# Feed-forward of a hybrid decoder layer: one set of PSUM tiles for both ways, weights loaded in quarters, a fifth room for stores, two operands of the way down loaded early

## The chip, the cores and the metric

The kernel runs on one core of a Trainium2 chip, in one launch. Its time is the device time in microseconds (us) of an execution, and the measure of a kernel is the median of its runs. A profile is one execution recorded by the hardware profiler; its span runs from the first to the last instruction.

## The reference, cut to what matters

One layer of a decoder works on 1024 prompt tokens and 8 sample tokens, each of 1024 features, in float32. A mixer (gated linear attention, a gated recurrence, windowed attention), cross-attention to a memory and a feed-forward block each add to `x`. The change lies in the last of them:

```python
D_MODEL, SEQ, DEC_BATCH, D_FF = 1024, 1024, 8, 4096

def ffn(x, g, w1, w2):
    h = rmsnorm(x, g) @ w1                      # 1024 -> 4096
    return jnp.square(jax.nn.relu(h)) @ w2      # 4096 -> 1024

xp = xp + ffn(xp, g_ffn[l], ffn_w1[l], ffn_w2[l])   # prompt
xs = xs + ffn(xs, g_ffn[l], ffn_w1[l], ffn_w2[l])   # sample
```

## The kernel before, in words

All tokens are taken together: N = 1032 columns, features on the partitions. A float32 product is made of three products of rounded operands: each operand is kept as a high and a low half (`halves`: ACT rounds the source into `hi`, DVE writes `lo = src - hi`), and TensorE adds `hi*hi`, `hi*lo` and `lo*hi` (`terms`).

The feed-forward runs in 30 units (`UNITS`). Hidden features 0 to 511 (the pairs p = 0 and 1 of 256 features) are computed plainly ahead of them, by `pl_cell`. Units 0 to 13 are the way up, one pair (p = 2 to 15) of hidden features each; units 14 to 29 are the way down, two (one for each half `dq` of the output features) for each of 8 chunks `c` of 512 hidden features. Both use a 2x2 scheme with seven products in place of eight, whose operands are named A11, S2, S1, A12, S3, S4, A21, A22 (weights and their sums) and B11, T2, B21, T1, T3, B22, T4 (data and its differences). The last names the steps too.

On the way up (`up_unit`) the 1032 columns form three groups of 344: the scheme makes two of them, in eleven groups of 12 products together with the third group, which is made plainly into `fe`. The results `fa` to `fg` go from PSUM to the cells `h` and three help cells in tile `gc` (ACT: relu and square; DVE: additions). Bank `fd` is filled by step S3, read by DVE and filled on by step A22. Each pair's `h` then gives seven operands for the way down; `h_store` splits each into halves in one of the rooms of `ST["ring"]` (two halves of a `q` tile, shown as `hst`, a part of a `v` tile, shown as `wsum`, and `MKV`) and stores it to DRAM (`hd`, 516 KB). A room is taken again when its last store has landed. For the last two pairs the ring has three rooms. `h_done` lists the stores of a pair: two are made in its own unit's step A22, five in the next unit through `bg_run`, which takes so many entries of a list at each step. The plain pairs' stores are spread over units 0 to 10 (`slow`).

On the way down (`down_unit`) the steps are A11, S2, A12, S1, S3, S4, A22, one operand each: `h_load` brings its two halves (516 KB each) from `hd` to a room of `RING`: parts of the operand tiles of the way up (`hs`, `ls`: shown as `xoph`, `xopl`) and of `XH`, `XL`, which come free as the last up unit ends. Each step has 24 products into tiles `a`, `b`, `c` or `d`. In the first chunk ACT copies a result to its place (`acc`, in tile `gc` at first, or `XT`), later DVE adds it there. A12 goes on with the tiles `a` of A11, S4 with `c` of S1, A22 with `d` of S3.

Weights: `unit_raw(n)` loads a unit's raw weights, 1 MB, to one of two tiles `wraw`; `unit_sums` makes the four sums on GpSimd (POOL); `prep(q)` splits one operand into halves (`wop`), five steps ahead (`LOOK`). The loads for unit n+1 are issued with the first split for unit n. All DMAs here are issued by SyncE (SP), in order. The program is ordered by Tile's scheduler; within an engine instructions run in that order.

PSUM: up to the last up unit there are tiles of four tags (`d`, `a`, `b`, `c`) in pool `psd`; ahead of unit 14 that pool is closed (`first_half.close()`) and pool `psy` opened over its place, with four tiles of two banks.

## Time and profile before

| | us |
|---|---|
| time of the kernel before, median of 3 runs | 1397.5 |
| lowest and highest run | 1393.65, 1398.03 |
| time of the profiled execution | 1394.97 |
| span of the profiled execution | 1393.3 |
| PE busy in it | 1322.7 |

The span is cut by the first product of each unit: `fa` on the way up, `a` on the way down. The first up unit begins at 745.77, the first down unit at 1051.35, the last at 1357.81. In a timeline row, the first number is the start, the second the duration, and the bracket at its end the time that the engine sat idle before it, with what ended that. DVE is VectorE, ACT ScalarE, PE TensorE, POOL GpSimd, SP SyncE, and SPq an issue of a DMA by SP. A row of a window has its start and end, its length, the busy time (and count of instructions) of PE, PE's weight loads, DVE, ACT and POOL, the granted clock as a share of full speed, the mean busy share of the 16 DMA engines, and GB/s. The helpers' lines are L141 (a product), L161 (ACT), L171 (DVE).

### The profile page before, as it was taken

What the parts mean: (1) busy time and instruction counts of PE and PEld (TensorE: products, weight loads), DVE (VectorE), ACT (ScalarE), POOL (GpSimd) and SP (SyncE); (2) the same over time, 40 slices, a digit from 0 to 9 for tenths busy, and PEclk for the clock granted to TensorE, in tenths of its full rate; (3) what the DMA queues carried; (4) which work ended last, traced back from release to release, by engine and by line L of the source; (5) the groups of instructions that cost most, each with busy time, mean ns of one, the idle gap of its engine ahead of it and who ended that gap; (6) DMA issues with size and microseconds to landing.
All of it is one profiled execution on the core that took longest, in us unless ns stands there. A gap on an engine that the chain in (4) does not pass through costs nothing.

```text
span 1393.3 us, 24517 instructions
## 1 busy us (share of the span) xinstructions
PE 1322.7 (95%) x9251; PEld 1216.9 (87%) x9251; DVE 1009.6 (72%) x1993; ACT 685.8 (49%) x1393; POOL 260.3 (19%) x245
## 2 busy tenths in 40 slices
PE   6999999999997989998999999999997999999998
PEld 4889888777876877786799999999997999999997
DVE  6276787667767664767698888878775577877785
ACT  5265455246476454555566676766664322222221
POOL 3000011400003101010004231322322223322310
PEclk9999999999998899998999999999999999999999
DMA  6114010201101444442243677676679988765624
GB/s 185 46 49 122 9 48 18 67 25 31 47 8 51 140 149 124 142 131 71 71 125 103 224 266 255 233 248 240 241 260 367 344 306 304 259 249 210 227 76 123
DMA packets 181022, 215.87 MB, mean 155 GB/s; under 512 B 26866, under 2 KB 114990, under 8 KB 180888
## 3 DMA queue, kind: packets, MB, share of 16 engines
q1 hardware_dynamic: 180264, 214.01, 45.8%
q8 instruction: 73, 1.20, 0.4%
q0 software_dynamic: 640, 0.30, 0.1%
q14 instruction: 45, 0.37, 0.1%
HBM read 145.28 MB, written 70.06 MB: 155 GB/s over the span
## 4 chain that ended last, share of the span: by engine, by line
PE 61%; DVE 17%; DMA 8%; ACT 8%; issue 4%; SPq 1%; POOL 0%; DVEq 0%; ACTq 0%; POOLq 0%
PE win L141 9%; PE a L141 7%; PE d L141 6%; PE c L141 6%; PE wo L141 6%; DMA hd<-hst 3%; PE b L141 3%; PE v L141 2%; PE f L141 2%; DMA hd<-wsum 2%; PE gx L141 2%; ACT hc L161 2%; DVE hc L171 2%; DVE hst L171 2%; PE wmo L141 2%
## 5 line engine op out<-in xcount | busy, mean ns | idle before, releaser
L1919 POOL TENSOR_TENSOR wsum<-wraw 128x512 f32<-128x512 f32 x60 | 86.7, 1445 | 389.1 <-DVE wop L171 312.2
L141 PE MATMUL win<-XL,wh 128*128 128x344 f32 x384 | 126.5, 330 | 0.0
L141 PE MATMUL win<-XH,wh 128*128 128x344 f32 x384 | 126.2, 329 | 0.2 <-ACT xy L161 0.2
L141 PE MATMUL win<-XH,wl 128*128 128x344 f32 x384 | 125.4, 327 | 0.0
L161 ACT ACTIVATE wh<-ws 128x512 fp32r<-128x512 f32 x130 | 79.9, 626 | 75.8 <-DMA ws<-in_w_out_dram 22.3
L141 PE MATMUL fe<-XH,wop 128*128 128x344 f32 x448 | 115.5, 321 | 0.0
L161 ACT ACTIVATE wop<-wsum 128x512 fp32r<-128x512 f32 x104 | 65.1, 626 | 97.7 <-PE d L141 29.8
L171 DVE TENSOR_TENSOR wl<-ws,wh 128x512 fp32r<-128x512 f32 x130 | 92.7, 725 | 28.0 <-ACT wh L161 23.3
L161 ACT ACTIVATE wop<-wraw 128x512 fp32r<-128x512 f32 x104 | 63.8, 625 | 96.7 <-PE b L141 32.7
L171 DVE TENSOR_TENSOR wop<-wsum,wop 128x512 fp32r<-128x512 f32 x104 | 80.5, 775 | 26.0 <-ACT wop L161 25.0
L171 DVE TENSOR_TENSOR wop<-wraw,wop 128x512 fp32r<-128x512 f32 x104 | 76.4, 735 | 10.1 <-ACT wop L161 9.5
L141 PEld LDWEIGHTS fe<-XH,wop 128*128 128x128 f32 x448 | 79.7, 190 | 0.0
L141 PEld LDWEIGHTS win<-XL,wh 128*128 128x128 f32 x384 | 72.2, 188 | 5.2 <-issue 3.9
L141 PEld LDWEIGHTS win<-XH,wl 128*128 128x128 f32 x384 | 72.3, 188 | 3.6 <-issue 2.7
L141 PEld LDWEIGHTS win<-XH,wh 128*128 128x128 f32 x384 | 72.2, 188 | 3.3 <-issue 1.9
L141 PE MATMUL fe<-XL,wop 128*128 128x344 f32 x224 | 71.9, 321 | 0.0
L141 PE MATMUL a<-XH,wop 128*128 128x258 f32 x352 | 67.6, 283 | 0.0
L141 PE MATMUL wo<-XH,wh 128*128 128x344 f32 x192 | 64.3, 335 | 2.2 <-ACT wh L161 2.2
L161 ACT ACTIVATE hc<-hc 128x344 f32<-128x344 f32 x126 | 61.3, 486 | 8.8 <-DVE hc L171 7.1
L141 PE MATMUL wo<-XH,wl 128*128 128x344 f32 x192 | 64.2, 334 | 1.0 <-DVE wl L171 1.0
L141 PE MATMUL wo<-XL,wh 128*128 128x344 f32 x192 | 63.0, 328 | 0.0
L141 PE MATMUL d<-XH,wop 128*128 128x258 f32 x320 | 60.8, 283 | 0.0
(547 smaller groups left out, 4123.9 us busy)
## 6 DMA issues: line engine op xcount, KB each, us to landing
wraw<-in_ffn_w_dram SPq DMA_DIRECT2D x60, 512.0 KB
hd<-hst SPq DMA_DIRECT2D x59, 516.0 KB
XH<-hd SPq DMA_DIRECT2D x36, 516.0 KB
XL<-hd SPq DMA_DIRECT2D x36, 516.0 KB
hd<-wsum SPq DMA_DIRECT2D x29, 516.0 KB
hd<-MKV SPq DMA_DIRECT2D x24, 516.0 KB
xoph<-hd SPq DMA_DIRECT2D x20, 516.0 KB
xopl<-hd SPq DMA_DIRECT2D x20, 516.0 KB
```

The costliest lines, as they stand in the source:

```text
L141: PE.matmul(out, lhsT, rhs, start=start, stop=stop, **kw)
L161: return ACT.activation(out, in_, func, **kw)
L171: return DVE.tensor_tensor(out, a, b, op=op)
L1919: POOL.tensor_tensor(o, a, b, op=op)
```

## The change

- PSUM: the first pool is closed ahead of unit 0, and four tiles of two banks, `Z["z"]`, serve the way up and the way down. On the way up `fa` takes tile 0, `fb`, `fc` and `fg` tile 1, `fe` tile 2, `fd` tile 3, each a bank of it in turn.
- Weights: `unit_raw` loads a unit's weights in four parts of 256 KB; `prep` issues them with the second to fifth split of the unit before instead of all with the first.
- Stores: a fifth room, of two `ws` tiles, from unit 1 on; a store from it is two DMAs of 258 KB. The last pair uses two rooms, the one before it three. On the way down two entries of the list of stores are taken at each step instead of one.
- Operands of chunk 0: B11 and T2 are loaded in unit 12 to a `q` and an `e` tile that are free by then; B21, T1, T3 and B22 in unit 13, T4 and three operands of chunk 1 in unit 14. The ring of rooms begins two operands later.
- The two output halves of chunk 0 are taken in the order 0, 1; the places of `acc` change with it. Three small tiles become one (`scales`), and `ws` tiles are 516 wide instead of 512.

```diff
-    UNITS = [...] + [("down", c, q) for c in range(NUNIT)
-                                                         for q in ((1, 0) if c == 0 else (0, 1))]
+    UNITS = [...] + [("down", c, q) for c in range(NUNIT) for q in range(2)]
...
-    def unit_raw(n):
+    def unit_raw(n, parts=range(4)):
...
-            for h in range(2):
-                SP.dma_start(r[:, 4 * h:4 * h + 4], w[:, 4 * h:4 * h + 4])
+            k = 2
...
-            for h in range(2):
-                SP.dma_start(r[:, 2 * h:2 * h + 2], w[:, 2 * h:2 * h + 2])
+            k = 1
+        for h in parts:
+            SP.dma_start(r[:, k * h:k * h + k], w[:, k * h:k * h + k])
...  prep(q)
-            if i == A11:
-                if n + 1 < len(UNITS):
-                    unit_raw(n + 1)
+            k = q - BASE[n]
+            if k == 0:
                 unit_sums(n)
+            elif k < 5 and n + 1 < len(UNITS):
+                unit_raw(n + 1, (k - 1,))
...  h_store(p, op, src)
-        ring_ = ST["ring"] if p < NPAIR - 2 else ST["ring"][:3]
+        ring_ = ST["ring"][:{NPAIR - 1: 2, NPAIR - 2: 3}.get(p)]
...
-        SP.dma_start(d, st.rearrange("p (s c) -> p s c", s=2))
+        if len(st) > 2:
+            SP.dma_start(d, v3(st[2], 2))
+        else:
+            for k in range(2):
+                SP.dma_start(d[:, k], st[k])
...  st_rooms()
-        ST["ring"] = [ST["q"][:, :N], ST["v"][:, 2048:2048 + N], ST["q"][:, N:], MKV]
+        ST["ring"] = [(x[:, :HALF], x[:, HALF:], x) for x in (ST["q"][:, :N], ST["q"][:, N:], ST["v"][:, 2048:2048 + N],
+                                                              MKV)]
...  up_unit(n)
-        def bank(f, name):
-            ps[name] = f(name)[:, :GW]
+        def bank(z, name):
+            h = Z["i", z] = 1 - Z.get(("i", z), 1)
+            ps[name] = Z["z"][z][:, 512 * h:512 * h + GW]
...
+            if n == 1 and i == A11:
+                ST["ring"].append([F("ws", HALF, "hst") for _ in range(2)])
+            if n == NPAIR - NPLAIN - 2:
+
+                if i == S2:
+                    for op, tag in ((B11, "q"), (T2, "e")):
+                        t = F(tag, 2 * N, "hfirst")
+                        HOP["r", op] = [v3(t[:, j * N:(j + 1) * N], 2) for j in range(2)]
+                elif i in (A12, A21):
+                    h_load(0, B11 if i == A12 else T2)
             if n == NPAIR - NPLAIN - 1:
 
-                for op in {S1: (B11, T2), S4: (B21,), A21: (T1,)}.get(i, ()):
+                for op in {S1: (B21, T1), S4: (T3,), A21: (B22,)}.get(i, ()):
                     h_load(0, op)
...  h_load(c, op)
-        kind, k, j = RING[(NOP * c + op) % len(RING)]
-        if kind == "x":
+        kind, k, j = RING[(NOP * c + op - 2) % len(RING)]
+        if (c, op) in ((0, B11), (0, T2)):
+            room = HOP["r", op]
+        elif kind == "x":
...  down_unit(n)
-        psP, psQ = (lambda name, tag=tag: psy.tile([128, 1024], F32, tag=tag, bufs=2, name=name)
-                    for tag in ("pr" if n % 2 else "rp"))
+        sets = [Z["z"][:2], Z["z"][2:]]
+        psP, psQ = sets[n % 2], sets[1 - n % 2]
...
-            bg_run(2 if k == 6 else 1)
+            bg_run(2)
...
-    for op in (T3, B22, T4):
-        at(d0, op - T3, lambda op=op: h_load(0, op))
+    at(d0, 0, lambda: h_load(0, T4))
...
-            at(*((d0 + 2 * c - 2 + n, k) if c > 1 else (d0 + 1, op)), lambda c=c, op=op: h_load(c, op))
+            at(*((d0 + 2 * c - 2 + n, k) if c > 1 or op > 1 else (d0, 2 + 3 * op)), lambda c=c, op=op: h_load(c, op))
...
-    psy = None
+    first_half.close()
+    psy = ctx.enter_context(tc.tile_pool(name="psy", bufs=1, space=bass.MemoryType.PSUM))
+    Z["z"] = [psy.tile([128, 1024], F32, name=f"z{i}") for i in range(4)]
     for n, u in enumerate(UNITS):
...
-        if n == d0:
-            first_half.close()
-            psy = ctx.enter_context(tc.tile_pool(name="psy", bufs=1, space=bass.MemoryType.PSUM))
```

## Rows read from the trace of the kernel before

**Rows 1.** The page: busy times, and PE's granted clock in 40 slices, in tenths.
```profile
PE 1322.7 (95%) x9251; PEld 1216.9 (87%) x9251; DVE 1009.6 (72%) x1993; ACT 685.8 (49%) x1393; POOL 260.3 (19%) x245
...
PEclk9999999999998899998999999999999999999999
```

**Rows 2.** Windows of units 5, 9, 12 to 15, 17; columns told above.
```profile
849.83:875.26 25.43, 22.72 (x135) 22.30 (x133) 21.20 (x32) 16.83 (x34) 6.85 (x5) 0.93 0.68 236
937.70:961.66 23.96, 21.02 (x134) 20.75 (x133) 19.25 (x28) 16.66 (x33) 6.22 (x4) 1.00 0.71 244
1003.29:1024.10 20.81, 20.81 (x134) 20.81 (x133) 16.91 (x24) 14.03 (x28) 7.69 (x5) 1.00 0.63 230
1024.10:1051.35 27.25, 21.23 (x134) 20.69 (x132) 18.50 (x28) 15.23 (x33) 6.03 (x5) 0.95 0.79 280
1051.35:1077.18 25.83, 23.95 (x178) 23.53 (x179) 15.43 (x21) 12.62 (x23) 6.17 (x4) 0.92 1.03 370
1077.18:1096.11 18.93, 18.93 (x161) 18.93 (x159) 8.02 (x11) 9.76 (x17) 4.61 (x4) 1.00 0.90 324
1116.24:1136.37 20.13, 20.13 (x170) 20.13 (x169) 15.53 (x23) 4.43 (x7) 5.17 (x5) 1.00 0.86 313
```

**Rows 3.** PE's waits from 745.7 on: us in total, times, longest.
```profile
PE fd L141 <- DVE hc L171: 6.4, 3, 2.9
PE a L141 <- ACT hc L161: 5.3, 1, 5.3
PE c L141 <- DMA xoph<-hd: 1.2, 1, 1.2
PE c L141 <- DMA xopl<-hd: 0.7, 1, 0.7
```

**Rows 4.** Timeline of unit 5: ACT and PE.
```profile
862.23 0.64 ACT L161 ACTIVATE hst<-hpl 128x516 fp32r<-128x516 f32 x1 [1.25 <-DMA hd<-hst]
863.86 0.64 ACT L161 ACTIVATE hst<-hc 128x516 fp32r<-128x516 f32 x1 [0.47 <-DMA hd<-hst]
...
869.87 0.40 PE L141 MATMUL fd<-XH,wop 128*128 128x344 f32 x1 [2.71 <-DVE hc L171]
```

**Rows 5.** ACT's waits for rooms in units 0 to 13.
```profile
ACT hst L161 <- DMA hd<-hst: 21.3, 13, 4.6
ACT wsum L161 <- DMA hd<-wsum: 16.4, 8, 3.5
...
ACT MKV L161 <- DMA hd<-MKV: 3.6, 4, 1.6
```

**Rows 6.** Timeline at the seam, ACT and PE, and of unit 14, ACT.
```profile
1049.42 0.63 ACT L161 ACTIVATE hst<-hc 128x516 fp32r<-128x516 f32 x1 [4.58 <-DMA hd<-hst]
...
1050.86 0.44 ACT L161 ACTIVATE hc<-fe 128x344 f32<-128x344 f32 x1
...
1051.35 0.58 PE L141 MATMUL a<-xoph,wop 128*128 128x258 f32 x1 [5.32 <-ACT hc L161]
...
1054.34 0.60 ACT L161 ACTIVATE gc<-a 128x516 f32<-128x516 f32 x1 [1.62 <-PE a L141]
...
1071.73 0.64 ACT L161 ACTIVATE hst<-hc 128x516 fp32r<-128x516 f32 x1 [2.66 <-DMA hd<-hst]
```

**Rows 7.** Timeline: issues of SP in units 5 and 13, POOL in unit 5.
```profile
861.06 2.00 SPq L1899 DMA_DIRECT2D wraw<-in_ffn_w_dram  x2
...
870.40 1.29 POOL L1919 TENSOR_TENSOR wsum<-wraw 128x512 f32<-128x512 f32 x1 [11.90 <-DVE wop L171]
...
1038.31 0.47 SPq L1959 DMA_DIRECT2D hd<-hst  x1
```

**Rows 8.** Window at the seam, with columns as in rows 2.
```profile
1044.00:1060.00 16.00, 10.68 (x69) 10.40 (x69) 8.85 (x13) 6.99 (x14) 5.70 (x4) 0.79 1.04 372
```

**Rows 9.** Timeline at the start of unit 0: PE, ACT.
```profile
745.77 0.32 PE L141 MATMUL fa<-XH,wop 128*128 128x344 f32 x1
...
746.40 0.44 ACT L161 ACTIVATE hpl<-f 128x344 f32<-128x344 f32 x1
```

More of the change, by code (lines that the diff above doesn't have):

```diff
@@ L513, in trunk_step @@
     spt = cst.tile([128, 4, 3], F32, name="spt")
-    qsc = cst.tile([128, 2], F32, name="qsc")
-    gkq = cst.tile([128, 2], F32, name="gkq")
-    gq8 = cst.tile([128, 2], F32, name="gq8")
+    scales = cst.tile([128, 6], F32, name="scales")
+    qsc, gkq, gq8 = (scales[:, i:i + 2] for i in (0, 2, 4))
     hgo = cst.tile([128, 3], F32, name="hgo")
@@ L1874, in trunk_step @@
     ST, HC, PL = {}, {}, {}
-    UNITS = [("up", p) for p in range(NPLAIN, NPAIR)] + [("down", c, q) for c in range(NUNIT)
-                                                         for q in ((1, 0) if c == 0 else (0, 1))]
+    UNITS = [("up", p) for p in range(NPLAIN, NPAIR)] + [("down", c, q) for c in range(NUNIT) for q in range(2)]
     RAW, SUM, OPS = {}, {}, {}
@@ L1888, in trunk_step @@
     BASE = [QUEUE.index((n, A11)) for n in range(len(UNITS))]
-    def unit_raw(n):
+    def unit_raw(n, parts=range(4)):
         u = UNITS[n]
-        if n < 2:
+        if n < 2 and parts[0] == 0:
             RAW["t", n] = F("q", 2048, "wraw")
@@ L2061, in up_unit @@
             if i == A11:
-                terms(bank(psA, "fa"), w, XOP[B11], True, False)
+                terms(bank(0, "fa"), w, XOP[B11], True, False)
                 with lift(LIFT_E):
                     act(p1, ps["fa"], AF.Copy)
-                terms(bank(psB, "fe"), w, XOP[GA][:4], True, False)
+                terms(bank(2, "fe"), w, XOP[GA][:4], True, False)
             elif i == A12:
@@ L2072, in up_unit @@
             elif i == S2:
-                terms(bank(psD, "fb"), w, XOP[T2], True, True)
+                terms(bank(1, "fb"), w, XOP[T2], True, True)
                 with lift(LIFT_E):
@@ L2076, in up_unit @@
             elif i == S1:
-                terms(bank(psD, "fc"), w, XOP[T1], True, True)
+                terms(bank(1, "fc"), w, XOP[T1], True, True)
                 with lift(LIFT_E):
@@ L2080, in up_unit @@
             elif i == S3:
-                terms(bank(psC, "fd"), w, XOP[T3], True, False)
+                terms(bank(3, "fd"), w, XOP[T3], True, False)
                 with lift(LIFT_E):
@@ L2086, in up_unit @@
             elif i == S4:
-                terms(bank(psD, "fg"), w, XOP[B22], True, True)
+                terms(bank(1, "fg"), w, XOP[B22], True, True)
                 with lift(LIFT_E):
@@ L2092, in up_unit @@
             elif i == A21:
-                terms(bank(psB, "fe"), w, XOP[GA][:4], True, False)
+                terms(bank(2, "fe"), w, XOP[GA][:4], True, False)
             else:
@@ L2133, in x_add @@
         tt(hv(XT[m], j), hv(XT[m], j), hv(ST["x", m], j), ADD)
+    Z = {}
     def y_rooms(dq):
@@ L2140, in y_rooms @@
                 XT[m], XT[m + 1] = t[:, :N], t[:, N:]
-            HC["acc", 1] = [HC["gt"][:, u * HALF:(u + 1) * HALF] for u in range(2)]
+            t = F("u", N, "acc")
+            HC["acc", 1] = [hv(t, u) for u in range(2)]
         else:
@@ L2146, in y_rooms @@
                 XT[m] = t[:, m * N:(m + 1) * N]
-            t = F("u", N, "acc")
-            HC["acc", 0] = [hv(t, u) for u in range(2)]
+            HC["acc", 0] = [hv(HC["gt"], u) for u in range(2)]
     def y_out(m, f):
-        p = f("yp")
+        p = f[m % 2]
         for h in range(2):
@@ L2211, in part, with banks @@
                       [(f32r(x[0])[:, k, cs], f32r(x[1])[:, k, cs]) for k in range(2)], start, stop)
-        def banks(f, name):
+        def banks(z, name):
             for u in range(2):
-                ps[name, u] = f(name)
+                ps[name, u] = z[u]
         for k, i in enumerate(seq(n)):
```

6 lines of the change are left out of this document (3 added, 3 removed).

## The prediction, written before the result

> **What bounds the kernel now.** Read the page first. PE is busy 95% of the span, and its granted clock stands at 9 tenths or more in all slices but the 13th, 14th and 19th, which lie in the first half, that the change leaves alone [rows 1]. So the kernel is PE's, and a change can only take away time in which PE waits, or in which it works at the lower of its two clock levels (1.2 instead of 2.4 GHz). Second, cut the feed-forward stage into its units [rows 2]. Units 0 to 13 are the way up, 14 to 29 the way down. Eleven of the fourteen up units last 20.81 us at a clock of 1.00 (unit 12 is shown), and a settled down unit lasts 20.13. The reader is to see which windows are longer:
>
> - unit 5: 25.43 - 20.81 = 4.62 us, at a clock of 0.93
> - unit 9: 23.96 - 20.81 = 3.15, at 1.00
> - unit 13: 27.25 - 20.81 = 6.44, at 0.95
> - units 14 and 15 together: 25.83 + 18.93 - 2 x 20.13 = 4.50, unit 14 at 0.92
>
> That is 18.7 us, and it is all that is to be had between the first up unit and the last down unit. Third, PE's waits in this stage [rows 3]: `fd` for DVE 6.4 in three waits, `a` for ACT 5.3, `c` for two loads 1.9, together 13.6. The other 18.7 - 13.6 = 5.1 us are time at the lower clock after a wait.
>
> Fourth, what stands behind each wait. In unit 5 ACT writes the high half of a store into a room of the ring and has to wait, 1.25 and then 0.47 us, until the room's last store has landed; everything behind it on ACT is late, DVE (which writes the low half) with it, and DVE reads bank `fd` so late that PE's next product into that bank starts at 869.87, after 2.71 us [rows 4]. Over the way up ACT waits 21.3 + 16.4 + 3.6 = 41 us for rooms, in 25 waits [rows 5]; most are hidden, two cost PE something. At the end of unit 13 the same thing is worse: ACT waits 4.58 us for a room, and behind it stands the read of bank `fe` at 1050.86, ended at 1051.30; the first product `a` of the way down starts at 1051.35 [rows 6]. `a` doesn't need `fe`: it waits since the second set of PSUM tiles takes the place of the first.
>
> **The change part by part.** The sum is made against the profiled execution: span 1393.3, time 1394.97 us, 1.7 around it.
>
> *Fifth staging (two `ws` tiles) and weights in four parts, units 1 to 12.* A store can now be five stores old before its room is needed. ACT's longest wait in these units is 3.5 us (the 4.6 is that of unit 13) [rows 5]; in a burst, stores stand 1 to 2 us apart, as the two at 862.23 and 863.86 [rows 4]. One more room is therefore worth about one such distance, and it takes waits of 1.25 and 0.47 us away whole and the longest to about 2. In unit 5, 1.7 us of ACT's lateness goes, and the weight issues, which hold SP for 2.00 us amid the stores [rows 7], can be passed by a store. I take both losses as gone: -4.6 and -3.1. The bounds: 0 (lateness only moves) and -7.8. The parts themselves cost nothing as long as POOL's sums are not late: POOL's sum at 870.40 was released by DVE's last read of the sums' room, not by the landing of weights [rows 7]. Each weight row is as long as before and the bytes are the same; the number of issues rises from 2 to 4 a unit, and of one store in five from 1 to 2. SP is not full in those units, so I put this at 0; the upper bound is a part that costs the queue as much as a whole transfer, 2 more x 1.4 us (priced below) a unit, which matters only where the queue is full, units 13 and 14: +5.7.
>
> Queued transfers of half a megabyte move 372 GB/s at a DMA share of 1.04 [rows 8]. The Trainium skill speaks against the splitting ("DMA: Bandwidth & Descriptors", section "Bandwidth": batch transfers to 1 MiB or more for three quarters of the peak). The fixed 2.0 us a transfer that the same page of the Trainium skill fits, for transfers that GpSimd issues, would make four parts 4.0 us dearer than two halves, an estimate, and the sum 8 us worse if units 13 and 14 both paid it. This case's trace disagrees for halves: at 372 GB/s no such fixed time is paid between them.
>
> *Four PSUM tiles kept throughout.* Every up product keeps two banks in turn, as before, and `fa` too; no wait can arise in the middle. At the seam `a` now goes to tiles 0 and 1, last read for `fa` and `fg`, and no longer waits for `fe`: -5.32, and with it the other 0.4 of unit 13's excess that is not the `fd` wait. -5.7. The wait of `fd` there (0.71) has the same three rooms as before: 0. The price comes earlier: the new tiles are made before unit 0, over banks that the plain products still hold. The last of these is read by ACT from 746.40 to 746.84, and `fa` starts at 745.77 [rows 9]. If the first up product waits for that read as `a` did for `fe`, +1.1; if its banks are others, 0. I take +1.1, because that is what the row at the other seam did.
>
> *Two operands of chunk 0 loaded in unit 12, the rest moved up.* B11 and T2 go to a free `q` and `e` tile, and unit 13 loads B21, T1, T3 and B22 in their place. The two loads that `c` waited for (1.9) are then asked for a whole unit before their use. With the lower clock that follows, units 14 and 15 lose 4.5 now; -4.5. Unit 12 takes four more transfers of 516 KB; at 372 GB/s [rows 8] one takes 528 kB / 372 = 1.42 us, so 5.7 us of queue in a unit of 20.81 us whose DMA share is 0.63 now [rows 2]: 0.63 + 0.27 = 0.90, hidden. If that cover were gone, unit 12's stores would land up to 5.7 us later, ACT would wait as in unit 13, and about 4 us (unit 5's loss) would return.
>
> *Two rooms for the last pair, stores two to a step.* This is where I expect a new wait. The operand loads hold SP's queue: a store issued at 1038.31 right behind them let ACT go on only at 1049.42, 11.1 us later [rows 6, 7]. In the changed kernel the queue holds, from the end of S1 in unit 13 (four of its eleven groups of products, 1024.10 + 4 x 1.89, about 1032): one store on its way, B21, T1, T3, B22 (8 transfers), three stores, and the weights (2 transfers' worth): 14 x 1.42 = 19.9, to about 1052. PE would begin unit 14 at 1024.10 + 20.81 + 0.71 = 1045.6. Pair 15's first two stores land at 1053.4 and 1054.8. With two rooms, its third store can be split on ACT only when the first has landed, 7.8 us into unit 14; queued behind that on ACT are the copies of `a` and on DVE the additions of `b`, and PE needs the first for A12, due 5.8 us (two steps of 20.13 / 7) into the unit. The wait is 0 if ACT's order has the copies first, and 7.8 + 0.6 (one copy [rows 6]) - 5.8 = 2.6 if not. Of the three later stores, the next pair can hold the copies of A12 and S1 in the same way, some 2 each. So 0 to 7.0, and up to 2.6 (units 14 and 15 now: 4.5 - 1.9) for the lower clock. I take +2.6: one such wait in full, nearest to the single wait of 2.66 us for a room that ACT has in unit 14 now [rows 6].
>
> The order of the two column halves of chunk 0, the merged `scales` tile and the 4 columns more in `ws` move no work: 0.
>
> Sum: -4.6 - 3.1 - 5.7 - 4.5 = -17.9, and + 1.1 + 2.6 makes -14.2, so 1394.97 - 14.2 = 1380.8. The profiled execution lies 2.5 under the median of 1397.5 (runs 1393.65 to 1398.03); part of that is likely the same chance waits on the way up, which the change takes away, so I carry half of it: 1382.
>
> **The rivals.**
>
> *The seam's wait moves into unit 14 in full.* For it: the queue is full there (DMA share 1.04 [rows 8]) and the rooms go from three to two. Against it: PSUM no longer ties PE to ACT's order as tightly, and the splits of weights are made five steps ahead. Price 7.0 + 2.6 instead of 2.6: 1387.8, or 1389 on the median's scale.
>
> *The fifth room doesn't do what it is for.* The waits of units 5 and 9 are two in fourteen, by chance of the order in ACT and DVE; ACT and DVE do the same work as before (21.2 of 25.4 us busy on DVE in unit 5 [rows 2]), so another order may be late in another unit. Then 7.8 isn't gained: 1388.5, or 1390. Both rivals together: 1395.5, or 1397, no change.
>
> *Slower: the two rooms pace the way down's first units.* If a store of pair 15 takes 11.1 us to land, as the one of 1038.31, and the copies always stand behind the next store on ACT, then the five stores left (three rounds of two rooms) take 3 x 11.1 = 33 us where a unit lasts 20.1, and what is left of the round reaches into unit 15: +13; with pauses as long as `a`'s each is followed by the lower clock, some 3 x 2 more, and the part transfers' +5.7 stretch the same queue. With the +1.1 that is 25.8, and -17.9 + 25.8 = +7.9: 1402.9. It decides from 11 us a round on; against it speaks that the queue is at 1.0 only for the first 8 us of the unit in my count and that loads of chunk 1 are now spread over two units.
>
> **How the numbers follow.** Forecast 0.52 (1376 to 1386 on either scale), wait in unit 14 in full 0.17 (to 1391), fifth room without effect 0.13 (to 1393), both 0.09 (1393 to 1398), slower 0.09. A measurement of this kernel can tell about 0.3%, 4 us, from no change. Faster by more than that holds the first two and most of the third, less a little for what I can't see in the order of the queues: 0.77; within 0.3%: 0.12; slower 0.11. The range runs from all 18.7 gained (1376.3, less one for the scale) to where 'both' begins: 1375 to 1395.
>
> **What would show it.** Right: up units 1 to 12 all at 20.8 and ACT's waits for rooms far below 41 us; no wait of `a` at the seam and unit 13 at about 21.5; no wait for operand loads; a first wait of `fa` near 1 us; in unit 14 one or two waits of PE for ACT or DVE of 1 to 3 us, with ACT held by a store's landing. Wrong: a wait of `fd` in other up units; a unit 14 over 25 us; PE waiting for weights or POOL on the way down.

## The result, and the profile after

| | before | after |
|---|---|---|
| median, us | 1395.63 | 1418.72 |
| lowest run, us | 1393.65 | 1416.65 |
| profiled execution, us | 1394.97 | 1418.94 |
| its span, us | 1393.3 | 1417.2 |

The ratio is 1.016, with a 95% interval of 1.0132 to 1.0188: the change makes the kernel slower by 23 us, where 1382 was forecast. One of its four runs took 2521.78 us, for a reason that isn't known, and is left out of the ratio. In 18 further kernels its parts were taken out or mended one by one; two of these are 0.7% faster than the kernel before (1383 us).

First the windows of after that answer to [rows 2]: units 0, 2, 5, 9, 12 and 13 of the way up, then 14, 15 and 17 (columns as there).

```profile
747.16:769.82 22.66, 21.16 (x132) 20.88 (x133) 15.92 (x20) 11.48 (x23) 11.01 (x7) 1.00 0.32 108
791.90:817.08 25.18, 22.65 (x133) 22.32 (x133) 18.49 (x28) 15.34 (x31) 7.22 (x5) 0.93 0.61 214
864.81:889.59 24.78, 22.61 (x133) 22.32 (x133) 19.21 (x27) 13.88 (x28) 5.96 (x5) 0.93 0.73 249
961.73:984.74 23.01, 21.07 (x134) 20.78 (x134) 17.94 (x25) 13.62 (x27) 4.96 (x5) 1.00 0.64 228
1033.21:1055.30 22.09, 21.04 (x133) 20.76 (x133) 17.25 (x22) 13.15 (x26) 6.38 (x5) 1.00 0.57 199
1055.30:1079.44 24.14, 21.34 (x135) 20.78 (x134) 17.10 (x27) 15.45 (x30) 1.92 (x2) 1.00 0.79 286
1079.44:1099.58 20.14, 20.14 (x170) 20.14 (x169) 16.41 (x20) 12.63 (x23) 5.88 (x4) 1.00 0.90 319
1099.58:1119.68 20.10, 20.10 (x170) 20.10 (x169) 9.44 (x13) 9.96 (x18) 5.56 (x4) 1.00 1.02 361
1139.81:1159.94 20.13, 20.13 (x170) 20.13 (x169) 16.17 (x23) 4.44 (x7) 7.63 (x7) 1.00 0.86 323
```

The way up is where the time went: 747.16 to 1079.44 is 332.28 us, against 305.58 before, +26.7. No up unit is settled any more. The way down begins without a loss: units 14 and 15 take 40.24 instead of 44.76, and from the seam (the start of unit 14) to the end of the span it is 337.8 instead of 341.9, -4.2. With a start 1.4 later the sum is +23.9, which is the difference of the spans.

Second, PE's waits of after from 740 on, which answer to [rows 3]: us in total, times, longest.

```profile
PE z L141 <- DVE gc L171: 23.8, 14, 2.5
PE z L141 <- ACT hc L161: 3.2, 3, 2.0
...
PE z L141 <- ACT hpl L161: 1.0, 1, 1.0
```

One wait for DVE in each of the 14 up units, 0.77 to 2.53 us. Together with the 3.2 they are 27.0 of the 41 us by which 332.28 is above 14 x 20.81. Most of the rest is lost after the waits: six of the units (two are shown) run at a clock of 0.93, part of the time at the lower of the two levels.

Third, the timeline of after, PE in units 0 and 2 (the first row answers to [rows 9]), and DVE ahead of the third row's wait.

```profile
747.16 0.43 PE L141 MATMUL z<-XH,wop 128*128 128x344 f32 x1 [0.96 <-ACT hpl L161]
755.38 0.43 PE L141 MATMUL z<-xoph,wop 128*128 128x344 f32 x1 [1.50 <-DVE gc L171]
801.39 0.42 PE L141 MATMUL z<-xoph,wop 128*128 128x344 f32 x1 [2.53 <-DVE gc L171]
...
795.79 1.78 DVE L171 TENSOR_TENSOR MKV<-hc,MKV 128x516 fp32r<-128x516 f32 x1
...
800.83 0.51 DVE L171 TENSOR_TENSOR gc<-z,gc 128x344 f32<-128x344 f32 x1
```

The waiting product is `fc` (step S1), and what it waits for is DVE's read of `fb` (`gc<-z` at 800.83, ended at 801.34). `fb` lies in the one bank of tile 1 and `fc` in the other. In unit 0 nothing of the way up has used the other bank yet, and still `fc` waits, 1.50 us, until `fb` has been read. So the wait is kept for the tile, not for the bank. The read itself is late since DVE takes store and weight subtractions first; one of them, at 795.79, takes 1.78 us where its like takes 0.69. Part four comes back to that row.

What was forecast and came: ACT's waits for rooms in the way up, the rows that answer to [rows 5], fell from 41.3 to 7.3 us; no wait at the seam, none for operand loads, none of `fd` in units 5 and 9.

```profile
ACT hst L161 <- DMA hd<-hst: 5.0, 5, 1.9
ACT MKV L161 <- DMA hd<-MKV: 1.2, 2, 0.6
ACT wsum L161 <- DMA hd<-wsum: 1.1, 2, 0.7
```

They are no proof of the fifth room, though: a PE that is late by 2 us a unit gives the stores 2 us more.

### The profile page after: what moved, and what is told of

It is laid out like the page before. It is cut to its first block, busy times and chain, and to the rows that moved or that the text cites. A ratio compares the mean times of both kernels' runs of the same rounds, so it can differ in the third digit from the quotient of the medians.

```text
span 1417.2 us, 24677 instructions
## 1 busy us (share of the span) xinstructions
PE 1333.8 (94%) x9251; PEld 1224.3 (86%) x9251; DVE 1023.2 (72%) x1993; ACT 689.2 (49%) x1393; POOL 262.0 (18%) x245
## 4 chain that ended last, share of the span: by engine, by line
PE 68%; DVE 18%; ACT 6%; issue 4%; DMA 3%; SPq 1%; POOL 1%; DVEq 0%; ACTq 0%; POOLq 0%
PE z L141 33%; PE win L141 9%; PE wo L141 6%; DVE hst L171 2%; PE v L141 2%; PE gx L141 2%; PE f L141 2%; DVE hc L171 2%; DVE wop L171 2%; PE wmo L141 2%; ACT hc L161 1%; DVE wl L171 1%; PE mx L141 1%; PE rgp L141 1%; DMA ws<-in_w_in_dram 1%
## 5 line engine op out<-in xcount | busy, mean ns | idle before, releaser
L141 PE MATMUL z<-XH,wop 128*128 128x258 f32 (+1 forms) x1984 | 421.6, 302 | 4.1 <-ACT hc L161 3.2
L141 PEld LDWEIGHTS z<-XH,wop 128*128 128x128 f32 x1984 | 328.4, 190 | 5.7 <-ACT hc L161 4.3
L141 PE MATMUL z<-XL,wop 128*128 128x258 f32 (+1 forms) x992 | 298.6, 301 | 0.0
L141 PE MATMUL z<-xoph,wop 128*128 128x258 f32 (+1 forms) x976 | 211.7, 302 | 23.8 <-DVE gc L171 23.8
L141 PEld LDWEIGHTS z<-XL,wop 128*128 128x128 f32 x992 | 189.1, 191 | 0.0
L141 PEld LDWEIGHTS z<-xoph,wop 128*128 128x128 f32 x976 | 162.9, 192 | 27.8 <-DVE gc L171 27.8
L141 PE MATMUL z<-xopl,wop 128*128 128x258 f32 (+1 forms) x488 | 146.4, 300 | 0.0
L171 DVE TENSOR_TENSOR XT<-XT,z 128x516 f32<-128x516 f32 x144 | 99.1, 690 | 42.4 <-PE z L141 39.2
L141 PEld LDWEIGHTS z<-xopl,wop 128*128 128x128 f32 x488 | 93.7, 192 | 0.0
L171 DVE TENSOR_TENSOR wop<-wraw,wop 128x512 fp32r<-128x512 f32 x104 | 82.2, 791 | 7.6 <-ACT wop L161 4.9
```

The lines of the kernel that those rows point to most:

```text
L141: PE.matmul(out, lhsT, rhs, start=start, stop=stop, **kw)
L171: return DVE.tensor_tensor(out, a, b, op=op)
```

## The experiments

**One: is it the tile?** Theory: `fc` and `fb` share a tile, and the wait goes with it. Rival: DVE is late whatever the place of `fc`, and the wait only moves. Four kernels.

`fc` in the other bank of `fd`'s tile:

```diff
-                terms(bank(1, "fc"), w, XOP[T1], True, True)
+                terms(bank(3, "fc"), w, XOP[T1], True, True)
```

> One word differs from the changed kernel: the result of step S1 (fc) goes to tile 3 instead of tile 1, so that fb and fc no longer share a tile. Theory (waits are kept per tile of two banks, not per bank): PE's waits for DVE's cells gc, 23.8 us in 14 waits, go to under 2, and with them the lower clock that follows (some 12 us); the waits for ACT's reads of fe (3.2 us) and the first one (1.0) stay; median 1380 to 1386. Rival (the way up is late since DVE itself is late, with five rooms and denser stores, whatever bank fc has): the 14 waits stay, median 1414 to 1420.

The whole change, but with the PSUM tiles of before (`psD`, `psA`, `psB`, `psC` up to the seam, then pool `psy`):

```diff
-                terms(bank(1, "fb"), w, XOP[T2], True, True)
+                terms(bank(psD, "fb"), w, XOP[T2], True, True)
...
+        if n == d0:
+            first_half.close()
...
```

> The changed kernel with the PSUM handling of the kernel before (two pools, tiles by tag), all the rest of the change kept. Theory: up units of 20.8 us without any wait of S1; units 5 and 9 without a wait for fd; a wait of 2 to 6 us at the seam for the last read of fe, since the second pool takes the first one's place again; median 1383 to 1390. Rival (DVE late by the new ring): a wait of 1 to 2.5 us in each up unit stays, median 1410 or more.

The kernel before with nothing but the four kept tiles (the lines on `Z["z"]`, `bank`, `sets` and `banks` of the diff):

> The kernel before with the four kept PSUM tiles alone. Theory: a wait at S1 in each of the 14 up units, 1 to 2.5 us, some with the lower clock behind them, no wait at the seam: median 1415 to 1428, since the ring waits of before come on top. Rival (DVE late by the new ring): no waits at S1, the seam's 5.3 us gained, 1386 to 1394.

The change with `fb`, `fc`, `fd`, `fe`, `fg` spread so that no product takes a tile just used, in a rotation over four units:

```diff
+        place = ((0, 2, 1, 3), (2, 3, 0, 1), (3, 1, 2, 0), (1, 0, 3, 2))[n % 4]
-        def bank(z, name):
-            h = Z["i", z] = 1 - Z.get(("i", z), 1)
+        def bank(z, name, h=0):
+            z = place[z]
...
-                terms(bank(1, "fc"), w, XOP[T1], True, True)
+                terms(bank(3, "fc"), w, XOP[T1], True, True)
...
```

> The changed kernel with the four tiles dealt out so that no product follows within two groups on a product into the same tile that still has to be read, over the seam too: per unit one tile for fa and the second fe, one for the first fe, one for fb and fd, one for fc and fg, the roles moving on from unit to unit. Theory: no wait on the way up but the first (about 1.0 us); seam and unit 14 without the old waits, but now, with PE at full pace, the two rooms of the last pair may hold ACT and cost 0 to 3 us in unit 14; median 1377 to 1382. Rival (DVE late): still waits of 1 us and more in most up units, over 1400.

Measured, us and ratio to the runs of the kernel before that were made beside it (medians 1393.64 to 1395.62), here and below: `fc` elsewhere 1397.01 (1.0013, 0.9993 to 1.0033), old PSUM 1393.17 (0.9998, 0.9977 to 1.0018), tiles alone 1407.24 (1.009, 1.0063 to 1.0116), rotated tiles 1394.05 (0.9998, 0.9982 to 1.0013). PE's waits from 740 on, of tiles alone:

```profile
PE z L141 <- DVE gc L171: 16.1, 14, 1.7
```

and of rotated tiles:

```profile
PE z L141 <- ACT hc L161: 7.4, 4, 4.9
PE f L141 <- DVE wl L171: 2.0, 1, 2.0
PE z L141 <- DVE gc L171: 2.0, 1, 2.0
```

(The last two of these lie outside the way up: `f` ahead of it, `gc` in unit 14.) The 14 waits come with the tiles alone, and go with one digit (`fc` elsewhere) or with the rotation. It is the tile; the rival falls. The tiles alone cost 13 us, less than was expected: the waits are shorter there (16.1 us against 23.8), the granted clock of the way up stays at 1.00, and the seam's wait is gone. The longer waits and the lower clock come only together with the rest of the change. But all three mended kernels are as fast as before, not 14 us faster. Of the forecast gain the seam's part is there; the way up still holds waits, and unit 8 of the rotated kernel is 27.47 us long. Its rows of SP, ACT and PE:

```profile
911.65 0.53 SPq L1960 DMA_DIRECT2D hd<-wsum  x1
...
918.49 0.64 ACT L161 ACTIVATE wsum<-hpl 128x516 fp32r<-128x516 f32 x1 [4.79 <-DMA hd<-wsum]
...
927.02 0.43 PE L141 MATMUL z<-xoph,wop 128*128 128x344 f32 x1 [4.87 <-ACT hc L161]
```

A store of a plain pair (`hpl`, ready for long) is written into a room whose last store was issued 7 us before, although there are five rooms: rooms are handed out in the program's order, and Tile's scheduler pulls the plain store ahead of its turn.

**Two: the terms one by one, on the rotated kernel.** Without the fifth room; with weights in halves; with three rooms and one store a step for the last pair; with the fifth room kept for plain stores alone.

```diff
-                ST["ring"].append([F("ws", HALF, "hst") for _ in range(2)])
```

> The change with its up products spread over the four tiles as in the run with rotated tiles (1394.1 us, profiled 1395.0), but without the fifth room: the ring keeps the four rooms of the kernel before. Prediction's reason (one more room is worth some 1.5 us of every wait for a room, and takes the long waits of PE away): the sum of ACT's waits for rooms in the way up rises from 30.2 us towards before's 41, and one or two more up units hold a wait of PE of 1 to 3 us: 1394.1 + 4.6 to 7.8 = 1398.7 to 1401.9. Rival (lateness only moves: which unit is late is set by the order in which ACT and DVE take the stores, and a fifth room changes that order as much as it helps): waits of PE in other units than 4, 5 and 8, the same sum within 3 us, 1391 to 1397.

```diff
...  unit_raw: two parts of 512 KB
-            elif k < 5 and n + 1 < len(UNITS):
-                unit_raw(n + 1, (k - 1,))
+                if n + 1 < len(UNITS):
+                    unit_raw(n + 1, range(2))
```

> The change with rotated tiles, but the raw weights of the next unit are asked for as two halves at the first step, as before, instead of four quarters at four steps. Prediction's reason (quarters let stores pass between them, and cost the queue nothing): stores that stand behind a whole unit's weights land later, ACT waits longer for rooms, and the long wait of unit 8 (4.8 us, behind quarters asked for at 907.2, 910.2, 910.7 and 912.2) stays or another takes its place: 1394 to 1399. Rival 1 (each quarter costs the queue a time of its own, worked out in the prediction as up to 5.7 us over the two units where the queue is full): 1388 to 1391, with DMA shares lower at equal bytes. Rival 2 (a store waits for the four quarters spread over the unit more often than for two halves at its start, which lie where no store is due): unit 8's wait goes, -4 to -6: 1388 to 1390, with fewer waits of ACT for rooms.

```diff
-        ring_ = ST["ring"][:{NPAIR - 1: 2, NPAIR - 2: 3}.get(p)]
+        ring_ = ST["ring"][:3 if p >= NPAIR - 2 else None]
...
-            bg_run(2)
+            bg_run(2 if k == 6 else 1)
```

> The change with rotated tiles, but the last pair keeps three rooms, and one store to a step, as before. Prediction's term (two rooms: 2.6 us, bounds 0 to 9.6; unit 14 of the run with rotated tiles is 4.7 us over a settled unit, with ACT held 4.6 us by a store's landing): unit 14 falls from 24.84 to 20.1 to 21.5, 1394.1 - 3.3 to 4.7 = 1389.4 to 1390.8. Rival (the queue, not the number of rooms: behind eight operand transfers any third or fourth store lands as late): ACT's wait moves by one store, unit 14 or 15 still holds a wait of PE of 2 to 3 us and a lower clock after it: 1393 to 1396.

```diff
-                ST["ring"].append([F("ws", HALF, "hst") for _ in range(2)])
+                ST["own"] = [F("ws", HALF, "hst") for _ in range(2)]
...  h_store(p, op, src)
+        if p < NPLAIN and "own" in ST:
+            st = ST["own"]
...
```

> The change with rotated tiles; the fifth room isn't one of the ring, but is kept for the stores of the plain pairs, which have been ready for long and are pulled ahead of their turn (one such, written into the ring's third room at 918.49, waited 4.79 us for a store issued in the same room 7 us before, and PE waited 4.87 us behind it). Theory 'order': a room handed out in program order but written ahead of its turn is a room just used; with a room of its own a plain store finds one that has been free for some 15 us. The wait of unit 8 and its lower clock go (27.47 to 20.8), and those of units 4 and 5 shrink: 1394.1 - 6.7 to 10 = 1384 to 1387.5; ACT's waits for rooms in the way up fall from 30.2 to under 20. Rival 'queue' (the rooms are late since the queue is, whoever asks): four rooms for the pairs' own stores are one fewer, the same sum of waits, 1392 to 1397. Prediction's reason (number of rooms): as without the fifth room, 1398 or more.

Measured: no fifth room 1394.69 (0.9995, 0.9977 to 1.0013), halves 1397.02 (1.002, 1.0003 to 1.0037), three rooms 1407.89 (1.0105, 1.0076 to 1.0133), own room 1393.38 (0.9994, 0.9975 to 1.0012). The fifth room is worth nothing that shows: "lateness moves". Quarters are worth about 3 us, at the edge of what these runs tell. Three rooms are no remedy for unit 14, on the contrary: ACT and PE there,

```profile
1076.35 2.08 ACT L161 ACTIVATE XT<-z 128x516 f32<-128x516 f32 x4 [7.12 <-DMA hd<-wsum]
...
1077.00 0.58 PE L141 MATMUL z<-XH,wop 128*128 128x258 f32 x1 [10.48 <-ACT XT L161]
```

the third room is a part of the `v` tile, and with the output halves now in the order 0, 1 the `XT` of unit 14 lies in that tile and waits for its last store. So the two rooms belong to the new order of the halves, which the prediction had put at nothing. (This run also makes one store a step instead of two; the two edits weren't tried apart.)

In the run with a room of their own the plain stores were all pulled into the first five units (DVE writes the last low half at 842.81, in unit 4). The windows of units 0 to 5 and of 6 to 12:

```profile
745.81:879.84 134.03, 128.56 (x793) 126.22 (x793) 114.25 (x156) 85.77 (x172) 38.11 (x24) 0.99 0.73 255
879.84:1026.13 146.29, 146.22 (x926) 145.39 (x926) 120.78 (x169) 97.10 (x196) 46.47 (x28) 1.00 0.64 228
```

The seven later units are 20.9 us each; the first six lose 9.2 us (134.03 - 6 x 20.81). DVE is busy 19.0 us a unit there, 17.3 later.

**Three: the stores in their order.** If rooms are the matter, then order cures it.

```diff
-        halves(hi, lo, src)
+        ins = act(hi, src, AF.Copy)
+        if "last" in ST:
+            tc.add_manual_dep(ins.ins, ST["last"].name, ORDER, reason="ring")
+        ST["last"] = ins.ins
+        tt(lo, src, f32(hi), SUB)
```

> The change with rotated tiles (1394.1 us), five rooms in the ring, and one thing added: on ACT each store comes behind the store before it in program order, so that a room is always used five stores after its last use. Theory 'order' (rooms are late since a plain pair's store is pulled ahead of its turn into a room just used): unit 8's wait of ACT of 4.8 us and PE's 4.87 behind it go, ACT's waits for rooms in the way up fall from 24.2 us (13.1 + 9.9 + 1.2) to under 12, units 4 to 9 come to 20.8 to 21.5: 1384 to 1388. Rival 'queue': stores land late whatever their order, the waits only sit elsewhere: 1392 to 1396, the sum of waits over 20 us.

The same with another rotation, `((0, 2, 1, 3), (2, 3, 1, 0), (3, 0, 1, 2))[n % 3]`:

> As the run with stores in order, and the rotation of the tiles changed so that no product is asked for a tile sooner than 5.7 us (three groups of products of 1.89) after its last reader in the unit before could begin: now the product of step S2 takes the tile whose last product was the second half of step A22's first group, and the product of S1 the tile of A22's second group; with the rotation so far S2's product had 3.8 us (two groups). If the rest of the waits in the up units (PE for ACT's reads, 0.2 to 2.8 us each) come from ACT's delay reaching over that slack, those below 1.9 us go and longer ones shrink by 1.9: 2 to 5 us less than the run with stores in order. Rival: with stores in order nothing is left of these waits, or DVE's read is as late as ACT's: the same within 2 us. Unit 14 is as in the rotated run (24.8, 4.7 us over).

That one with later operand loads:

```diff
-                for op in {S1: (B21, T1), S4: (T3,), A21: (B22,)}.get(i, ()):
+                for op in {S1: (B21,), A21: (T1,)}.get(i, ()):
...
-    at(d0, 0, lambda: h_load(0, T4))
+    for k, op in enumerate((T3, B22, T4)):
+        at(d0, k, lambda op=op: h_load(0, op))
```

> As the run with other places, and of chunk 0's operands only B21 is asked for in step S1 of unit 13; T1 follows in A21, T3, B22 and T4 in the first three steps of unit 14. The trace of the rotated run has at 1041.82 two stores behind four operand transfers, and ACT held 4.63 us at 1053.20 until the first of them had landed. Theory 'queue' (the two rooms cost what stands ahead of the stores): with two transfers fewer ahead (2 x 1.42 us) ACT is held 1.8 us or less, PE's waits in unit 14 (0.65 and 1.97, then the lower clock) go or nearly: unit 14 from 24.8 to 20.1 to 22, 3 to 4.7 us less than the run before it. Rival: T3 and B22, asked for some 10 us before their use behind weights and stores, are late themselves: PE waits for a load in unit 14 for 1 to 4 us, the time is the same or 2 us more.

Stores in order, but with four rooms (no `append`):

> Stores in order, rotated tiles, but four rooms in the ring as before the change. The prediction's reason (one more room is worth a store's distance, 1.5 us a wait, 7.7 us in all): 4 to 8 us more than the run with stores in order and five rooms, ACT's waits for rooms twice that run's. Rival (once the stores are in order, four rooms are enough, and the fifth does nothing that shows): the same within 2 us.

Measured: in order 1397.3 (1.002, 1.0002 to 1.0037), other places 1395.84 (1.0001, 0.9986 to 1.0015), later loads 1396.49 (1.0011, 0.9994 to 1.0028), four rooms 1392.41 (0.9971, 0.9955 to 0.9987), the first that is faster than before, by 0.3%. ACT's wait for rooms in the whole way up, with four rooms in order (the kernel before, with four rooms too, had 41.3 [rows 5]):

```profile
ACT hst L161 <- DMA hd<-hst: 0.4, 1, 0.4
```

and PE's waits in the same stretch of the same run:

```profile
PE z L141 <- ACT hc L161: 3.4, 4, 1.3
PE z L141 <- DVE hc L171: 2.2, 4, 0.9
```

Here the prediction's main reason falls. The waits for rooms are gone, the up units still take 300.0 us, 8.7 above 14 x 20.81; in the kernel before, without the 5.7 of the seam, it was 8.5. "Order" was right on the rooms and wrong on the time. Other places change who waits, not the sum. Later loads bring the forecast rival: PE waits 1.6 and 1.0 us for `XH` and `XL` in unit 14. That five rooms in order take 5 us more than four isn't explained; 3.8 of them are one wait of 2.0 us in unit 1, with the lower clock after it.

**Four: work or queue?** On the kernel with four rooms in order: the plain pairs' splits and differences left out, with the same transfers; the same work on POOL instead of DVE; the last pair's low halves there too; all pairs' differences there.

```diff
+        if p < NPLAIN:
+            for k in range(2):
+                SP.dma_start(d[:, k], src)
+            return
```

> As the run with stores in order and four rooms (1392.4 us), but the two plain pairs' stores aren't split and their differences aren't formed: the products' operands of chunk 0 that come from them are stored as they are, twice, so the queue carries the same bytes, and ACT and DVE have none of the work (14 copies of 0.63 us on ACT, 14 subtractions for the low halves and 8 for the differences on DVE, 0.69 us each). It leaves out this part of the computation. Theory 'work in bursts' (with no wait for a room left, PE still waits 0.2 to 1.3 us in eight up units for DVE and ACT, since a plain store and its difference come on top of a unit that fills DVE 17 of 20.8 us by itself): the waits go, every up unit from the first to the last comes to 20.8 to 21.0, their sum from 300.0 to 291.5 to 294: 1384 to 1386.5. Rival 'queue' (what is late is the landing of what the queue carries, which is the same): the up units keep 300 us within 2, the time 1391 to 1394.

```diff
+        if p < NPLAIN:
+            POOL.tensor_tensor(lo, src, f32(hi), op=SUB)
+        else:
+            tt(lo, src, f32(hi), SUB)
```

> As the run with stores in order and four rooms, but the low halves and the differences of the two plain pairs are computed on POOL instead of DVE: 22 subtractions, 15 us less for DVE over the way up, and some 22 x 1.7 = 37 us more for POOL, which is busy 6.5 of 21 us a unit. Theory 'work in bursts': waits of PE for DVE go, those for ACT's reads shrink since ACT waits less for DVE: 4 to 8 us less, 1384.5 to 1388.5. Rival (POOL is slow: a difference takes it 1.7 us, the weights' sums come behind it and are late, or ACT's copies alone make the burst): PE waits for weights or for ACT, 1391 to 1396.

> As the run before it, and the low halves of the last pair's stores on POOL too, so that DVE isn't held when ACT waits for a room in unit 14. Theory (what PE waits for there, 0.18 us for ACT's copy and 2.54 us for DVE's addition of product b, is DVE behind the held store): the 2.54 us and the lower clock after it go, unit 14 from 24.9 to 20.5 to 22: 3 to 4.5 us less than the run before it. Rival (ACT's copies stand behind the same held store, and POOL's halves take 1 us longer, so rooms come free later): unit 14 stays over 23.5, no gain.

> As the run with the plain pairs on POOL, and the four differences of every later pair on POOL too: DVE loses 4 x 0.69 = 2.8 us a unit more (17 to 14 us), POOL gains 4 x 1.7 = 6.8 us (13.3 of 20.8). Theory 'work in bursts', taken further: no wait of PE for DVE in the way up, 0 to 3 us less than the plain pairs alone. Rival (the chain, not the share: each difference ends 1 us later, the stores behind it too, and the pair's two buffers come free later for the next pair): waits of PE for ACT and DVE grow, 1 to 6 us more.

Measured: unsplit 1387.79 (0.9946, 0.9925 to 0.9966), plain pairs on POOL 1399.8 (1.0041, 1.0025 to 1.0056), last pair too 1400.53 (1.005, 1.0032 to 1.0068), all differences 1432.02 (1.0274, 1.0248 to 1.0301). Without the plain pairs' work the way up takes 295.51 us, 4.5 less. This doesn't rule the queue out, though: stores that wait for no split are issued early, the last nine of them from 743.07 on, as the way up begins (749.41). These issues by SP, and the window of the way up:

```profile
743.07 8.01 SPq L1961 DMA_DIRECT2D hd<-hpl  x9
...
749.41:1044.92 295.51, 293.05 (x1848) 290.98 (x1849) 225.63 (x325) 187.79 (x382) 88.03 (x56) 1.00 0.64 226
```

At 226 GB/s against the 243 of four rooms in order the way up itself moves some 6 MB less. Part five decides this. But work taken from DVE and given to POOL makes the kernel slower. The window of the way up, first of four rooms in order, then of plain pairs on POOL, shows why:

```profile
747.99:1048.02 300.03, 294.00 (x1849) 290.81 (x1849) 239.41 (x347) 195.07 (x395) 91.09 (x56) 1.00 0.69 243
```

```profile
745.98:1053.71 307.73, 296.48 (x1848) 290.76 (x1849) 243.29 (x329) 195.00 (x395) 119.48 (x76) 1.00 0.67 236
```

DVE has 18 operations fewer and is busy 3.9 us longer. Its operations became slower. The timeline of DVE, then of POOL, in the run with four rooms in order:

```profile
921.12 1.29 DVE L171 TENSOR_TENSOR hst<-hc,hst 128x516 fp32r<-128x516 f32 x1 [0.28 <-ACT hst L161]
922.88 1.23 DVE L171 TENSOR_TENSOR wop<-wsum,wop 128x512 fp32r<-128x512 f32 x1 [0.48 <-ACT wop L161]
924.03 1.78 DVE L171 TENSOR_TENSOR hc<-hc 128x516 f32<-128x516 f32 x1
...
927.45 0.68 DVE L171 TENSOR_TENSOR wsum<-hpl,wsum 128x516 fp32r<-128x516 f32 x1
...
929.87 0.50 DVE L171 TENSOR_TENSOR gc<-z,gc 128x344 f32<-128x344 f32 x1
...
920.56 1.30 POOL L1918 TENSOR_TENSOR wsum<-wraw 128x512 f32<-128x512 f32 x1 [15.43 <-DVE hc L171]
921.93 1.63 POOL L1918 TENSOR_TENSOR wsum<-wsum,wraw 128x512 f32<-128x512 f32 x1
923.53 1.74 POOL L1918 TENSOR_TENSOR wsum<-wraw 128x512 f32<-128x512 f32 x1
925.22 1.75 POOL L1918 TENSOR_TENSOR wsum<-wraw,wsum 128x512 f32<-128x512 f32 x1
```

While POOL forms the four weight sums, one behind the other, a subtraction of two SBUF tiles takes DVE 1.2 to 1.8 us; at 927.45, when POOL has ended, 0.68. It is so over the whole way up of this run: no such subtraction takes more than 0.70 us clear of POOL's sums, and the 73 that overlap one take 1.09 in the mean. How this reaches PE stands in unit 7 of the same run (DVE, ACT, PE):

```profile
898.41 1.78 DVE L171 TENSOR_TENSOR hc<-hc 128x516 f32<-128x516 f32 x1
...
900.23 0.63 ACT L161 ACTIVATE hst<-hc 128x516 fp32r<-128x516 f32 x1 [3.64 <-DVE hc L171]
...
902.16 0.42 PE L141 MATMUL z<-xoph,wop 128*128 128x344 f32 x1 [1.34 <-ACT hc L161]
```

ACT waits for the slow subtraction, reads PSUM late behind it, and PE waits for that read. The Trainium skill ("SBUF — State Buffer", section "SBUF: two separate sides") says that a DVE operation with two SBUF inputs and a GpSimd operation that reads SBUF take the same shared pair of ports, each for its whole length, while the other stands still. The durations here agree in that both sides grow longer; whole operations in strict turn would take 0.68 + 1.30 = 1.98 us a pair, and the last two sums above start 1.6 and 1.7 us after the one before them.

**Five: the sums apart, or on DVE.** If a burst on POOL sets DVE back by more than the products' slack, then spreading the four sums helps at the same work, and moving them to DVE helps although DVE then has more to do. If DVE's total counts, the first does nothing and the second harms.

```diff
...  unit_sums(n)
+        if k == 4:
+            s3, s4 = s1, s2
+            SUM["later"] = {2: (s4, a12, s2, SUB), 3: (s3, a11, a21, SUB)}
+            todo = todo[:2]
...  prep(q)
+            if UNITS[n][0] == "up" and k in (2, 3):
+                o, a, b, op = SUM["later"][k]
+                POOL.tensor_tensor(o, a, b, op=op)
```

> As the run with stores in order and four rooms (1392.4 us), but POOL forms a unit's four weight sums not in one go: the first two at the step where all four were formed, the fourth a step after the second has been split, written over it, and the third a step after the first has been split, written over that. In the trace of the run with four rooms a subtraction of 128x512 or 128x516 takes DVE 0.68 us at 927.45 to 930.89, and 1.01 to 1.78 at 921.12 to 926.52, while POOL's four sums run one behind the other (920.56 to 926.97); the additions that read PSUM take 0.50 us in both. Theory 'POOL slows DVE': in the 6.7 us of a burst of sums DVE falls some 4 us behind, which is more than the slack of the up products that follow, and PE waits; with two bursts of 3.4 and single sums of 1.7 us DVE falls behind 2 us at most: the waits in the up units (8.6 us over 14 units against 291.4) fall by half or more: 1385 to 1389. Rival (only DVE's total counts, 17.1 of 20.8 us a unit, and the same sums slow as many of its operations): 1391 to 1394.

```diff
-            POOL.tensor_tensor(o, a, b, op=op)
+            (DVE if 0 < n < NPAIR - NPLAIN else POOL).tensor_tensor(o, a, b, op=op)
```

> As the run with stores in order and four rooms (1392.4 us), but the weight sums of units 1 to 13 are formed on DVE instead of POOL. Theory 'POOL slows DVE': every subtraction on DVE takes 0.68 us, the mean of those that write hc (0.897), wop (0.836, 0.704) and the store rooms (0.80) falls to 0.68 to 0.70; DVE gains 4 x 0.68 = 2.7 us a unit and loses about 1.3 of slowed work, 18.5 of 20.8. A burst of four sums sets it back 2.7 us instead of 4: the waits shrink a little: 1387 to 1392. Rival (DVE's total is what counts): 1.4 us a unit more on the engine that is late already: waits of PE for DVE in most units, 1394 to 1402.

Measured: sums apart 1383.2 (0.9927, 0.9909 to 0.9945), sums on DVE 1383.44 (0.9924, 0.9908 to 0.9939), both faster than was expected. By the ratios that is 6 us less than with four rooms in order. The way up of sums apart, then of sums on DVE:

```profile
746.16:1038.73 292.57, 292.57 (x1849) 292.56 (x1849) 237.32 (x345) 201.30 (x395) 82.41 (x57) 0.99 0.71 249
```

```profile
749.47:1040.48 291.01, 291.01 (x1848) 291.01 (x1849) 241.10 (x399) 198.82 (x395) 6.73 (x4) 1.00 0.72 251
```

PE waits nowhere inside the way up; PE's busy time is the length of the window (the first has 1.6 us of lower clock in unit 0, after 3.5 us of waiting ahead of it). With the sums on DVE that engine has 52 operations more than with four rooms in order and is busy 1.7 us longer, and the 8.7 us are gone all the same. With sums apart DVE's subtractions lose as much beside POOL as before (77 overlap a sum, 1.07 us in the mean): only the time of the loss is another. "Total" falls, "burst" stands. The queue falls here too: these two ways up move as many bytes as that of four rooms in order (about 73 MB each, by the GB/s of the windows) and hold no wait. Both edits also change the order of work on DVE; none of the other orders tried here had a way up without waits. That either edit alone, on the kernel before, would do as much wasn't tried.

Both still lose in unit 14: with sums apart it lasts 24.87 us, at a clock of 0.93. DVE and PE there:

```profile
1044.60 1.78 DVE L171 TENSOR_TENSOR hc<-hc 128x516 f32<-128x516 f32 x1
1046.29 1.80 DVE L171 TENSOR_TENSOR hst<-hc,hst 128x516 fp32r<-128x516 f32 x1
1048.02 1.75 DVE L171 TENSOR_TENSOR wop<-wraw,wop 128x512 fp32r<-128x512 f32 x1
...
1050.42 0.39 PE L141 MATMUL z<-xoph,wop 128*128 128x258 f32 x1 [2.55 <-DVE gc L171]
```

ACT is held 4.39 us by a room (the two-room wait of the prediction), DVE behind it, and then DVE's next operations fall into the four sums of the down unit, which are still in one go. In the run with the last pair's low halves on POOL the wait for DVE was gone from unit 14, which took 23.12 us, but 1.1 and 0.5 us of waits for ACT and 0.6 for a load had come in, and unit 15 lost 1.1.

## Why the prediction was wrong, point by point

- **"Every up product keeps two banks in turn, as before, and `fa` too; no wait can arise in the middle."** This step failed, and it decides the sign. Two banks of one tile are not two tiles. Rotated tiles against the change as it is: 1394.05 against 1418.72, ratios 0.9998 and 1.016, about 23 us. The prediction counted banks where the kept wait goes by tiles. It had a hint: "as `a` did for `fe`" at the seam [rows 6] is also a wait for a place and not for data, and it drew the consequence for `fa` alone.
- **Fifth room and quarters, -4.6 and -3.1.** Wrong in the mechanism. ACT's waits for rooms stood ahead of PE's wait in unit 5 [rows 4], and were taken for its whole cause. With those waits gone altogether PE still lost 8.7 us on the way up. The rival "the fifth room doesn't do what it is for" was the right one, at 0.13; what it lacked was the reason, which in the kernels with four rooms in order is DVE slowed by POOL's sums. For the quarters' price the value taken, 0, holds within some 3 us, on the better side. [Rows 7] were read for what POOL waits for, not for what POOL does to DVE. In unit 5 of the kernel before, POOL stood idle for 11.90 us up to 870.40 [rows 7], all through PE's wait; there the sums could only act through work left over from earlier. How much of the waits of its units 5 and 9 was the rooms' and how much DVE's stays open.
- **Seam, -5.7.** Right: no wait there in any run with the kept tiles, and in the one with the old PSUM it came back with 3.4 us. It is the one gain of the forecast that the traces show.
- **Operand loads, -4.5.** No wait for a load in units 14 and 15 of the change, as forecast. But without PE's lateness the two rooms take the place: unit 14 is 4.7 us over in the rotated run, where 2.6 was put (bounds 0 to 9.6). The net of the two is 0. In the change itself unit 14 cost nothing; that PE came to it 28 us later is a likely reason, which wasn't tested.
- **First `fa`, +1.1.** 0.96 measured, for the read that was named [rows 9].
- **The order of the two column halves, put at 0.** True of the change as built; but by the trace it is what makes PE wait 10.48 us with three rooms.
- **Slower, 1402.9, at 0.09.** The sign came with another mechanism in another place; units 14 and 15 were settled.

So with the PSUM step mended (rotated tiles, 1394.05) the forecast of 1382 is still 12 us too low. By the profiles, both with a span of 1393.3: the way up of rotated tiles takes 302.66 us instead of 305.58, -2.9 where -13.4 was forecast; from the seam on it is +0.5 where -1.9 was; and unit 0 starts 2.5 later where 1.1 was, of which 1.5 come from a part that the change leaves alone. Most of the gap is the term of 7.7 us for room and quarters, which wasn't there.

## What to carry to other kernels

When PSUM tiles are merged, count the waits by tile: a product into a tile whose other half is still to be read waited here, whichever bank it wrote. A wait that stands ahead of another in the trace isn't its cause until a run without the first has lost the second. And look along POOL's rows for what they do to DVE's durations: the same subtraction at 0.68 and at 1.78 us in one timeline tells more than either engine's share.

## What the runs showed of the hardware

DVE's subtractions with both sources in SBUF take 0.68 us alone and up to 1.80 beside POOL's sums (four rooms in order, sums apart); POOL's sums 1.30 at the start of a burst and 1.63 to 1.75 beside DVE's. Additions that read PSUM keep 0.50. Moving 22 operations from DVE to POOL, 18 of them within the way up, raised DVE's busy time there by 3.9 us. That a trade between two engines can cost both was not expected here.

PE's waits of about 2 us had two outcomes: in after, unit 9 has one of 1.95 us and keeps a clock of 1.00 (23.01 us long), unit 5 one of 2.17 and has 0.93 (24.78).
